# One pool of PSUM banks for matrix products and transposes beside the attention of a two-layer decoder trunk

## The chip, the cores and the metric

The kernel runs on one core of one Trainium2 chip. The metric is the device time of one execution in microseconds (us); three executions of the kernel before took 2252.82, 2257.99 and 2261.49 us, so its median is 2257.99 us.

## What is computed

Two layers (DEPTH 2) work on 1024 tokens of width 1024. Cut to what matters here, a layer is:

```
u   = x * (1 + scale) + shift
A, B, C inputs, gates and merge logits = u W_in
A: GLU -> depthwise conv(31) -> LayerNorm -> swish, times SiLU(A_gate), -> W_a_out = y_a
B: Bg * conv3(Cg * xb), times SiLU(B_gate), -> W_b_out = y_b
C: causal attention of 8 heads on low-rank q and kv, times SiLU(C_gate), -> W_c_out = y_c
m   = sum_i sigmoid(merge_i) * y_i
x   = LayerNorm(alpha * x + gate * (m W_o))
```

The attention of a head is softmax(q k^T * scale) v with a causal mask. All large products are made from a high and a low part of each operand, as three matmuls of 512 columns for each 128 rows of the sum.

## The kernel before, in words

Everything is held transposed (channels on the 128 partitions, tokens along the free axis) and cut into two halves of 512 tokens, h = 0 and h = 1. Each layer has three phases, and `phase` (L1177) closes the PSUM pool and opens it again with another layout at each. Phase 0 makes the large input products and the convolutions. Phase 1 is the attention of the first half of the tokens, beside the output products of the branches B and A of that half. Phase 2 is the attention of the second half; beside it lie the C products of the first half (`merge_jobs`, tile `yps`, L1034), the products with W_o (`wo_jobs`, tile `ops`, L1091), the LayerNorm of the first half (`ln_jobs`, L1094) and the B and A products of the second half. The two phases with attention are the ones that the change touches.

The attention of a head and half (`att_jobs`, L873) has four kinds of jobs. A score job (L904) makes one 128-query block of scores in a bank of tag `st`, takes its maximum on VectorE (L919), the exponential on ScalarE (L921) and divides by the sum (L922, L923), which gives the tile `prob`. A flip job (L928) takes one bank of tag `tp` (tile `tps`), transposes three or four 128x128 blocks of `prob` into it on TensorE (L938), and `split` copies the bank out as a high part on ScalarE (L129) and a low part on VectorE (L130), tile `pt`. A values job (L947) multiplies `pt` with V into the one bank of tag `av` (tile `avps`, L954), which is held for a whole head. A finish job (L958) adds up and gates the head. A head has 3 flips in phase 1 and 7 in phase 2, so the two layers have 2 x 8 x (3 + 7) = 160.

The products beside it take one bank of tag `pj` each (`chunk`, L164): a `yps` product has 12 matmuls and is read by VectorE (L1025 for B, L1028 for A and C), an `ops` product has 24 and is read by VectorE at L1049. The LayerNorm of a half takes a bank of tag `tp` for the mean (tile `meanps`, L757), which eight VectorE instructions read one after the other (L762), then one of tag `tp` for the variance (tile `qv`, L530) and one of tag `av` for the factor that is applied (tile `rstd`, L545). The A products of the second half wait for this LayerNorm: their inputs `y` (loaded at L1003, split at L132 and L133) lie in the buffers c0 to c3, and these are free only when the LayerNorm has been applied (L1103, L1109) and stored.

The order of the jobs is written out by hand: `blend` (L89) mixes attention jobs and product jobs by their estimated costs, `weave` (L66) spreads the LayerNorm jobs over the products (L1248 to L1256). That is the order of the calls. The Tile framework then orders the instructions of each engine ahead of time, by its own estimates, so that TensorE can take a ready product ahead of a transpose that stands earlier in the order of the calls. Within one tag, though, the banks are given out in the order of the calls: in the program before, the tiles on each bank follow one another in that order. A tile that finds no free bank of its tag waits until the last reader of one is done.

The layouts of the phases give each tag its number of banks, eight in all; a score tile of phase 2 takes two banks:

```
layouts = (dict(pj=3, sd=3, tp=1, av=1), dict(pj=3, st=2, tp=2, av=1), dict(pj=2, st=2, tp=1, av=1))
```

Of the kernel before, what the change touches and what calls it, by code (L numbers as in the profile page):

```python
# [1285 lines left out]
def trunk(nc, tc, *args):  # L1286
    from contextlib import ExitStack
    with ExitStack() as es:
        mk = lambda name, **k: es.enter_context(tc.tile_pool(name=name, **k))
        bufs = dict(tab=1, wr=6, ws=6, tt=1, sp=2, ab=2, w=6, x=2, n=5, sm=8, acc=1)  # L1290

        class Pool:
            def __init__(self, p):
                self.p = p

            def tile(self, shape, dt, tag, name):
                return self.p.tile(shape, dt, tag=tag, name=name, bufs=bufs.get(tag, 1))
        class Banks:

            layouts = (dict(pj=3, sd=3, tp=1, av=1), dict(pj=3, st=2, tp=2, av=1), dict(pj=2, st=2, tp=1, av=1))  # L1300
            stack = None

            def lay_out(self, n):
                if self.stack is not None:
                    self.stack.close()
                self.stack = es.enter_context(ExitStack())
                self.bufs = self.layouts[n]
                self.p = self.stack.enter_context(tc.tile_pool(name="ps", bufs=1, space=PSUM))

            def tile(self, shape, dt, tag, name):  # L1310
                return self.p.tile(shape, dt, tag=tag, name=name, bufs=self.bufs[tag])
        big = Pool(mk("a", bufs=1))
        pools = (mk("const", bufs=1), Pool(mk("w", bufs=1)), big, big, Banks(),
                 mk("dram", bufs=1, space=DRAM))
        Trunk(nc, tc, pools, args[:-1], args[-1]).build()
# [74 lines left out]
```

## Time and profile before

| what | value |
|---|---|
| median of three executions | 2257.99 us |
| the profiled execution's own time | 2257.43 us |
| span of its instructions | 2254.8 us |
| mean granted TensorE clock | 0.977 |
| TensorE (PE) busy | 95% |
| VectorE (DVE) busy | 80% |
| ScalarE (ACT) busy | 50% |
| phases 1 and 2 of layer 0 | about 735 to 1062 us, then products alone |
| phases 1 and 2 of layer 1 | about 1850 to 2160 us, then products alone |

PE is matmul work, PEld the loading of weights, which overlaps it. The granted clock is the share of full speed that TensorE was given. A row of the view of waits says which instruction of an engine waited for the end of which other one, for how long in total, how often, and the longest time. A matmul that writes into a bank and waits for the VectorE instruction that reads the bank last is a wait for a bank.

### The profile page before, as it was taken

Reading aid. Unit: us, or ns where it says so; the run is one execution under the profiler, and the core shown is the slowest. Engines: PE = TensorE matmul, PEld = TensorE weight load, DVE = VectorE, ACT = ScalarE, POOL = GpSimd, SP = SyncE. Lnnn points to the kernel's source line nnn. Section 1 sums busy time; section 2 is a strip of 40 time slices with the busy share of each in tenths; the row PEclk is TensorE's granted clock in tenths of the full one; section 3 lists DMA queues with packets and bytes.
Section 4 is the critical chain, followed back from the end, with each engine's and each line's share of the span. In section 5 each row is a group of like instructions: output and inputs, shape, how many; then the busy total and the mean of one; then the engine's idle time right before and its main releaser. Section 6 shows DMA issues by size and latency. Waiting matters only on the chain.

```text
span 2254.8 us, 29755 instructions
## 1 busy us (share of the span) xinstructions
PE 2139.8 (95%) x10097; PEld 1723.9 (76%) x10097; DVE 1810.3 (80%) x2910; ACT 1138.4 (50%) x2072; POOL 235.6 (10%) x483
## 2 busy tenths in 40 slices
PE   8889999999999989988997999999999999999896
PEld 7668788888778778866775787888887778887686
DVE  4786889899997788787868769899898868867786
ACT  2764443343443756655448544443434447666743
POOL 4010100000001321101001101000000023211000
PEclk9999999999999999997998999999999999999998
DMA  7575642223224986665535757332222269745442
GB/s 265 180 203 189 186 167 100 97 99 103 79 72 125 238 228 187 175 193 173 178 108 189 201 163 207 119 107 89 94 69 67 68 197 221 190 129 141 159 156 64
DMA packets 185191, 336.68 MB, mean 149 GB/s; under 512 B 22608, under 2 KB 47440, under 8 KB 185040
## 3 DMA queue, kind: packets, MB, share of 16 engines
q1 hardware_dynamic: 124560, 218.50, 31.2%
q0 software_dynamic: 46656, 91.12, 15.4%
q10 hardware_dynamic: 13824, 25.17, 3.0%
q8 instruction: 79, 1.29, 0.2%
q14 instruction: 72, 0.59, 0.1%
HBM read 254.16 MB, written 80.54 MB: 148 GB/s over the span
## 4 chain that ended last, share of the span: by engine, by line
PE 75%; issue 11%; DMA 5%; DVE 4%; ACT 3%; POOL 1%; SPq 0%; POOLq 0%; DVEq 0%; ACTq 0%
PE lgps L295 19%; PE bgps L295 7%; PE xgps L295 7%; PE aps L295 7%; PE cgps L295 3%; PE agps L295 3%; PE yps L186 3%; PE yps L187 3%; PE yps L188 3%; PE avps L954 3%; PE tps L938 3%; PE ops L186 2%; PE score L914 2%; PE ops L187 2%; PE ops L188 2%
## 5 line engine op out<-in xcount | busy, mean ns | idle before, releaser
L295 PE MATMUL lgps<-u,wsplit 128*128 128x512 f32 x2016 | 483.9, 397 | 13.7 <-ACT lgps L260 12.0
L295 PEld LDWEIGHTS lgps<-u,wsplit 128*128 128x128 f32 x2016 | 379.8, 189 | 108.3 <-ACT lgps L260 13.8
L129 ACT CAST wsplit<-wraw 128x512 fp32r<-128x512 f32 (+1 forms) x524 | 318.3, 615 | 270.7 <-DVE wraw L220 54.8
L130 DVE TENSOR_TENSOR wsplit<-wraw,wsplit 128x512 fp32r<-128x512 f32 (+1 forms) x524 | 353.5, 679 | 71.2 <-ACT wsplit L129 67.8
L736 DVE SCALAR_TENSOR_TENSOR cacc<-abuf,vec,cacc 128x1024 f32<-128x1024 f32 x240 | 306.9, 1279 | 0.6
L295 PE MATMUL xgps<-u,wsplit 128*128 128x512 f32 x672 | 160.4, 397 | 0.0
L295 PE MATMUL bgps<-u,wsplit 128*128 128x512 f32 x672 | 160.0, 397 | 0.0
L295 PE MATMUL aps<-u,wsplit 128*128 128x512 f32 x672 | 158.1, 395 | 0.0
L295 PEld LDWEIGHTS xgps<-u,wsplit 128*128 128x128 f32 x672 | 126.0, 188 | 31.6 <-issue 1.4
L295 PEld LDWEIGHTS bgps<-u,wsplit 128*128 128x128 f32 x672 | 126.0, 188 | 31.5 <-issue 1.4
L295 PEld LDWEIGHTS aps<-u,wsplit 128*128 128x128 f32 x672 | 126.2, 188 | 30.6
L130 DVE TENSOR_TENSOR pt<-tps,pt 128x512 fp32r<-128x512 f32 (+1 forms) x160 | 100.9, 634 | 36.9 <-ACT pt L129 35.8
L129 ACT CAST pt<-tps 128x512 fp32r<-128x512 f32 (+1 forms) x160 | 85.7, 540 | 77.2 <-PE tps L938 74.8
L954 PE MATMUL avps<-pt,Vh 128*128 128x256 f32 x640 | 120.5, 303 | 1.7 <-ACT pt L129 1.2
L919 DVE TENSOR_REDUCE nm<-score 128x1 f32<-128x384 f32 (+7 forms) x128 | 95.8, 751 | 30.8 <-PE score L917 30.2
L186 PE MATMUL yps<-y,wsplit 128*128 128x512 f32 x256 | 107.4, 422 | 12.4 <-ACT y L132 6.2
L921 ACT ACTIVATE prob<-score,nm 128x384 f32<-128x384 f32 (+7 forms) x128 | 94.3, 740 | 46.0 <-PE tps L938 25.0
L186 PE MATMUL ops<-m,wsplit 128*128 128x512 f32 (+1 forms) x320 | 114.8, 359 | 0.0
L188 PE MATMUL ops<-m,wsplit 128*128 128x512 f32 (+1 forms) x320 | 112.8, 353 | 0.0
L187 PE MATMUL ops<-m,wsplit 128*128 128x512 f32 (+1 forms) x320 | 112.6, 352 | 0.0
L938 PE MATMUL tps<-cs,prob 128*128 128x128 f32 x576 | 93.1, 279 | 18.0 <-DVE pt L130 17.5
L954 PEld LDWEIGHTS avps<-pt,Vh 128*128 128x128 f32 x640 | 95.6, 195 | 14.2 <-ACT pt L129 7.4
(322 smaller groups left out, 4253.9 us busy)
## 6 DMA issues: line engine op xcount, KB each, us to landing
wraw<-in_win SPq DMA_DIRECT2D x264, 256.0 KB, 2.7
wraw<-in_wout SPq DMA_DIRECT2D x96, 256.0 KB, 3.0
mt<-tD SPq DMA_DIRECT2D x96, 256.0 KB, 4.4
adaraw<-in_wada SPq DMA_DIRECT2D x64, 256.0 KB, 3.3
wraw<-in_wo SPq DMA_DIRECT2D x64, 256.0 KB, 3.0
tD<-mt ACTq DMA_DIRECT2D x48, 256.0 KB, 2.0
Kh<-knD POOLq DMA_DIRECT2D x48, 256.0 KB, 5.1
Vh<-vD POOLq DMA_DIRECT2D x48, 256.0 KB, 5.7
```

The costliest lines, as they stand in the source:

```text
L129: nc.scalar.copy(dst[:, 0], src)
L130: nc.vector.tensor_tensor(dst[:, 1], src, dst[:, 0].bitcast(F32), op=ALU.subtract)
L186: mm(ps, w[:, 0, c], x[k][:, 0, cols], start=k == 0, stop=False)
L187: mm(ps, w[:, 0, c], x[k][:, 1, cols], start=False, stop=False)
L188: mm(ps, w[:, 1, c], x[k][:, 0, cols], start=False, stop=k == n - 1)
L295: mm(ps, w[:, a, c], x[:, e], start=n < 2 and k == 0 and i == 0, stop=k == 3 and i == 2, skip_group_check=True)
L736: nc.vector.scalar_tensor_tensor(acc, a[:, k:k + S], w, acc, op0=ALU.mult, op1=ALU.add)
L914: mm(o, q[0:96, 0, qc], k[0:96, 0, :w], start=True, stop=False)
L919: nc.vector.tensor_reduce(nm[:, 0:1], sp[:, :nk], axis=AX.X, op=ALU.max, negate=True)
L921: nc.scalar.activation(p[:, :nk], sp[:, :nk], AF.Exp, bias=nm[:, 0:1], accum_out=nm[:, 1:2])
L938: nc.tensor.transpose(tp[:, c:c + P], st["p", hd, 2 * half + b][:, (2 * kp + k) * P:(2 * kp + k + 1) * P], self.ident)
L954: mm(av[:, half * 256:(half + 1) * 256], v[:, 2 * kp + k], pt[:, w, (1 - k) * 256:(2 - k) * 256], start=kp == 0 and k == 0 and w == 0, sto ...
```

## The change

In the two layouts with attention the tags `pj` and `tp` become one tag of as many banks as the two had together: 3 + 2 = 5 in phase 1, 2 + 1 = 3 in phase 2. A request for a tag that the layout does not have (`tp`) is served from `pj`. Phase 0 keeps its layout. No instruction is added or removed.

```diff
-            layouts = (dict(pj=3, sd=3, tp=1, av=1), dict(pj=3, st=2, tp=2, av=1), dict(pj=2, st=2, tp=1, av=1))
+            layouts = (dict(pj=3, sd=3, tp=1, av=1), dict(pj=5, st=2, av=1), dict(pj=3, st=2, av=1))
             stack = None
@@
             def tile(self, shape, dt, tag, name):
+
+                tag = tag if tag in self.bufs else "pj"
                 return self.p.tile(shape, dt, tag=tag, name=name, bufs=self.bufs[tag])
```

## Rows read from the trace of the kernel before

**Rows 1.** Stretches: length, busy PE, PEld, DVE, ACT, POOL (instructions), granted clock, DMA share, GB/s.
```profile
735.00:845.00 110.00, 100.22 (x553) 82.24 (x554) 82.67 (x172) 71.57 (x170) 34.16 (x75) 0.95 0.90 234
845.00:945.00 100.00, 99.00 (x557) 82.16 (x557) 81.19 (x139) 63.74 (x112) 15.94 (x34) 1.00 0.70 186
945.00:985.00 40.00, 32.39 (x173) 26.27 (x172) 29.40 (x49) 20.35 (x36) 4.58 (x10) 0.97 0.66 174
985.00:1010.00 25.00, 22.15 (x117) 17.00 (x116) 20.77 (x41) 14.05 (x25) 1.41 (x3) 0.91 0.59 189
1010.00:1060.00 50.00, 40.33 (x185) 32.93 (x185) 36.93 (x68) 31.54 (x50) 6.35 (x13) 0.76 0.51 163
...
1850.00:1938.00 88.00, 86.81 (x489) 71.53 (x490) 69.45 (x149) 63.71 (x156) 29.48 (x65) 0.96 0.94 229
1938.00:2060.00 122.00, 120.10 (x664) 99.33 (x665) 86.01 (x143) 78.48 (x137) 19.58 (x41) 1.00 0.57 152
2060.00:2110.00 50.00, 47.65 (x252) 36.61 (x251) 40.79 (x70) 32.17 (x56) 4.89 (x11) 1.00 0.49 140
2110.00:2135.00 25.00, 18.02 (x84) 13.84 (x83) 18.99 (x32) 18.73 (x32) 1.38 (x3) 0.80 0.49 158
```

**Rows 2.** Waits of PE, 725 to 1110 us (layer 0): total, times, longest.
```profile
PE tps L938 <- DVE pt L130: 10.0, 7, 3.3
PE yps L186 <- DVE mt L1028: 6.1, 1, 6.1
PE yps L186 <- DVE mf L1025: 5.4, 1, 5.4
PE score L914 <- ACT prob L921: 5.3, 5, 2.4
...
PE score L914 <- DVE gt L795: 1.4, 1, 1.4
```

**Rows 3.** Waits of PE, 1845 to 2255 us (layer 1).
```profile
PE tps L938 <- DVE pt L130: 7.5, 7, 3.3
...
PE yps L186 <- DVE mt L1028: 2.4, 2, 1.4
...
PE avps L954 <- ACT pt L129: 1.2, 2, 0.9
```

**Rows 4.** Busy time by stretch of the transposes' instructions (tile tps) alone, without POOL.
```profile
971.00:989.00 18.00, 0.00 (x0) 0.22 (x1) 0.00 (x0) 0.00 (x0) 0.82 0.45 113
...
2071.00:2082.00 11.00, 0.00 (x0) 0.00 (x0) 0.00 (x0) 0.00 (x0) 1.00 0.19 39
```

**Rows 5.** Timeline, 1026 to 1036 us: consecutive transposes and their copies (start, us).
```profile
1027.74 0.59 ACT L129 CAST pt<-tps 128x512 fp32r<-128x512 f32 x1 [3.94 <-PE tps L938]
1028.36 0.69 DVE L130 TENSOR_TENSOR pt<-tps,pt 128x512 fp32r<-128x512 f32 x1 [1.89 <-ACT pt L129]
...
1029.10 1.12 PE L938 MATMUL tps<-cs,prob 128*128 128x128 f32 x4 [0.76 <-DVE pt L130]
...
1033.91 0.87 PE L938 MATMUL tps<-cs,prob 128*128 128x128 f32 x3 [3.27 <-DVE pt L130]
```

**Rows 6.** Groups of instructions, 735 to 1062 us: busy, mean ns, idle before.
```profile
L923 ACT ACTIVATE prob<-prob,nm 128x128 f32<-128x128 f32 (+3 forms) x64 | 48.0, 774 | 5.4 <-DVE nm L922 5.4
L919 DVE TENSOR_REDUCE nm<-score 128x1 f32<-128x128 f32 (+3 forms) x64 | 47.8, 750 | 14.3 <-PE score L917 14.0
...
L921 ACT ACTIVATE prob<-score,nm 128x128 f32<-128x128 f32 (+3 forms) x64 | 47.2, 740 | 27.5 <-PE tps L938 13.6 <-DVE nm L919 13.6
L130 DVE TENSOR_TENSOR pt<-tps,pt 128x512 fp32r<-128x512 f32 (+1 forms) x74 | 46.5, 632 | 13.0 <-ACT pt L129 12.6
L938 PE MATMUL tps<-cs,prob 128*128 128x128 f32 x268 | 44.1, 283 | 10.0 <-DVE pt L130 10.0
L129 ACT CAST pt<-tps 128x512 fp32r<-128x512 f32 (+1 forms) x74 | 39.6, 540 | 35.9 <-PE tps L938 35.5
...
L1028 DVE SCALAR_TENSOR_TENSOR mt<-mt,yps 128x512 f32<-128x512 f32 x19 | 13.0, 684 | 3.5 <-PE yps L188 2.7 <-DMA mt<-tD 0.8
```

## The prediction

> **What bounds the kernel now.** I read the busy time by stretch first [rows 1]. TensorE is the engine to save: in the stretches up to 945 us in layer 0 and up to 2060 us in layer 1 it is busy for 91 to 99% of the time. It falls off later in phase 2: 32.4 of 40 us, 22.2 of 25, 40.3 of 50 in layer 0, and 47.7 of 50 and 18.0 of 25 in layer 1. Over these five stretches 7.6 + 2.8 + 9.7 + 2.3 + 7.0 = 29.4 us are idle, and in three of them the granted clock is 0.91, 0.76 and 0.80, so that part of the work ran at 1.2 instead of 2.4 GHz right after such idle time.
>
> The view of waits then says what TensorE waited for. The first row of either layer is the same: a transpose waits until VectorE has read the bank of the transposes before, 10.0 us in 7 waits and 7.5 us in 7 [rows 2, 3]. That is a wait for a bank, since `pt` itself lies in four other buffers. The timeline shows one turn of the single `tp` bank of phase 2: four transposes, the ScalarE copy (0.59 us), the VectorE copy (0.69), and the next transposes only after that [rows 5]. From one ScalarE copy to the transposes that follow it are 1.36 us; with the transposes ahead of it (0.87 to 1.12 us here) the bank turns in some 2.4 us when nothing is late. A head has 7 flips in phase 2, so 17 us of the 27 us that a head has (217 us from 845 to 1062, by 8) go through this one bank at the least.
>
> Something is late, though. The mean of the LayerNorm takes the same bank, and in 18 us of layer 0 and 11 us of layer 1 not one transpose runs [rows 4]. TensorE passes that time with products of branch B, which stand later in the order of the calls. Then these run out, as the A products wait for the LayerNorm, whose `qv` stands in the queue for the same bank behind the transposes held up, and whose `rstd` waits for the `avps` bank of a head that is late for the same reason. The stretches after it, 1010 to 1060 and 2110 to 2135 us, are the worst of all.
>
> **The change, part by part.** It adds and removes no instruction and no DMA, so the sum is about waits alone.
>
> *Phase 1* goes from 3 + 2 banks to 5. The transposes hardly lacked a bank there: in 1850 to 1938 us TensorE is busy for 86.8 of 88 us [rows 1]. One wait of a product for its bank, 6.1 us at the end of phase 1 in layer 0 [rows 2], could profit from banks that no flip needs any more. I take it with the product waits below.
>
> *Phase 2, transposes.* With three banks the turn of one bank no longer sets the pace of the flips; the next thing late is a copy, at 0.54 us on ScalarE and 0.63 on VectorE per flip [rows 6], or the softmax. The bank waits of 17.5 us bound the gain from above. From below I bound it at nothing, as each could become a wait for the copy (like the 1.2 us of the values in layer 1 [rows 3]) or for the softmax (5.3 us in layer 0 [rows 2]). I take 60%, -10.5 us: nearer to the upper end, because the waits for this bank are nearly three times the others.
>
> *Phase 2, products.* They waited 6.1 + 5.4 + 2.4 = 13.9 us for a bank [rows 2, 3]. A third bank lets one more product start, but while the mean holds one bank of the three, two are left, as before, and the flips now want them too. Bounds: 0 and -13.9; I take -3, near the lower end, for VectorE is what is late behind the 5.4 us.
>
> *The clock.* The time lost to the lower level is at most the idle share of the clock times the busy time: 0.24 x 40.3 + 0.09 x 22.2 + 0.20 x 18.0 = 15.3 us [rows 1]. If about half of the idle time goes, I expect half of this back: -7.5 (bounds 0 and -15.3).
>
> *What the shared tag costs.* Within a tag the banks are given out in the order of the calls. So a product can no longer start ahead of a transpose that stands before it; it waits until that transpose has its `prob`. The trace before has no such wait. The nearest rows are the two stretches without a transpose: products and other work kept TensorE busy in the 18 us less the 5.4 us of the wait inside, and in the 11 us [rows 2, 4], 23.6 us together. If all of that stood still the cost would be +23.6; if the flips are ready when their turn comes it is nothing. In the stretch after the mean, though, the transposes start 0.05 us after the copy that frees the bank (28.36 + 0.69 against 29.10 [rows 5]), so their `prob` lay ready. I take +4. The queues behind: VectorE and ScalarE are in order, and copies of flips now come in groups of up to three, which is in the 60% above.
>
> *The borders of the phases.* Banks lie elsewhere after the change, so the first scores wait for another tile of phase 0; the one such wait is 1.4 us [rows 2]. I take 0, between -1.4 and +1.4, as phase 0's last gates cover it.
>
> Sum: -10.5 - 3 - 7.5 + 4 + 0 = -17.0 us. The profiled execution took 2257.4 us, which is 0.6 below the median of the three, so 2240.4 and, on the median, **2241 us**.
>
> **The rivals.** *No change, 27%: the banks were not it.* Each bank wait becomes a wait for the copy or the softmax, and VectorE, busy for 37 of the 50 us from 1010 [rows 1], is what is late. Then a fifth of the transposes' waits goes (-3.5) and the clock stays: 2254 us. For it: the 5.4 us of a product are VectorE's lateness. Against it: the flips lined up behind one bank, and ScalarE waited 35.5 us for transposes before its copies [rows 6]. A measured case of the Trainium skill speaks for this rival ("TensorE: Matmul & The Clock Gate", section "HAM oscillation — how this bites in real kernels"): double-buffering PSUM gave a kernel with long sums no further gain (125.5 against 126.6 us). By that rule the time here would stay at 2258. It fits the products, whose 12 or 24 matmuls outlast the 0.68 us of their read [rows 6], not the flips, whose three or four transposes at 0.28 us are over before the two copies of 0.54 and 0.63 are.
>
> *Slower, 15%: products queue behind transposes that are not ready.* Place: the start of each head, in both phases with attention. The softmax of a block after its scores takes 0.75 + 0.74 + 0.77 us for maximum, exponential and division [rows 6], 2.26 us; today TensorE fills that with a product. There are 2 x 2 x 8 = 32 heads, 72 us if nothing fills it. Scores and values still fill most. It decides from 17 / 32 = 0.53 us of unfilled time per head; at 1 us per head it is +32 - 17: 2273 us. Against it: phase 1 with its two banks for flips had the same softmax to wait for, and TensorE was at 99% there in layer 1 [rows 1].
>
> *Much faster, 8%.* All waits for banks go, the LayerNorm comes early enough for the A products, and the clock holds: -17.5 - 6 - 15 = 2219 us.
>
> *The change does not do what it says:* two of the three banks always hold products and one is left for flips, which is the layout before. It gives 2258 and lies in the 27%.
>
> **How the numbers follow.** The forecast of a gain through the free bank has 50%, with a range of its own of 2228 to 2250 us. The range that is to hold 8 in 10 leaves out the upper half of the slower case and the lower part of the much faster one: 2218 to 2266. A measurement of this kernel can tell 0.5%, 11.3 us, from no change: faster is below 2246.7, slower above 2269.3. Faster: most of the 50%, the 8% and a little of the 27%, 0.57. Slower: the 15% and a tail of the order in which the framework lays the instructions anew, which I can't work out, 0.17. Same: 0.26.
>
> **What would show it.** Right: the waits of `tps` for `pt` are down by more than half in both layers; transposes run while the mean is read; the span from the mean to the factor of the LayerNorm is shorter; the clock after 1010 us is above 0.9. The 60% is wrong if waits of the values for `pt` or of scores for `prob` take the place of the bank waits. The +4 is wrong if TensorE shows waits ahead of products for `prob`, or idles at the start of each head. The forecast as a whole is wrong if phase 2 is no shorter though the bank waits have gone, or if phase 1, which has nothing to gain, grows.

## The result, and the profile after

The changed kernel takes 2232.03 us (median of four executions, 2226.85 to 2233.02) against 2255.89 us for the kernel before in the same sessions (2252.82 to 2261.49): a ratio of 0.9897 with a 95% interval of 0.9879 to 0.9916, or 23.9 us less. The profiled executions have spans of 2230.0 and 2254.8 us, 24.8 us apart. That is faster by more than 0.5%, inside the range, and inside the forecast's own range of 2228 to 2250 us; the gain was forecast at 17 us.

Where it came from is read from the busy time by stretch, cut at the same events in both runs: the first score of a layer, the end of the last head of phase 1, the first read of the LayerNorm's mean, the end of the last head of phase 2, the last read of a product (each taken from the first and last instructions of the tiles `score`, `avps`, `meanps` and `yps`). Columns as in [rows 1]. The kernel before, nine stretches from the first score of layer 0 on:

```profile
735.90:821.60 85.70, 82.91 (x481) 68.66 (x482) 66.68 (x146) 62.22 (x153) 30.96 (x68) 0.98 0.92 233
821.60:971.80 150.20, 140.89 (x768) 115.91 (x767) 116.53 (x197) 87.79 (x152) 22.52 (x48) 0.98 0.73 197
971.80:1078.60 106.80, 88.83 (x433) 70.04 (x431) 80.52 (x143) 58.00 (x96) 8.39 (x18) 0.86 0.55 170
1078.60:1104.10 25.50, 25.50 (x114) 20.59 (x114) 23.11 (x41) 10.67 (x18) 0.00 (x0) 1.00 0.61 196
1104.10:1845.60 741.50, 719.82 (x3090) 571.93 (x3088) 617.55 (x902) 343.59 (x598) 47.30 (x89) 0.99 0.40 127
1845.60:1933.10 87.50, 84.09 (x481) 69.63 (x482) 67.12 (x147) 62.44 (x153) 31.10 (x69) 0.96 0.93 229
1933.10:2071.50 138.40, 135.49 (x740) 111.16 (x739) 100.16 (x163) 86.76 (x152) 22.43 (x47) 1.00 0.60 159
2071.50:2160.80 89.30, 79.88 (x416) 61.93 (x416) 67.61 (x116) 58.13 (x97) 4.05 (x10) 0.94 0.44 140
2160.80:2188.90 28.10, 26.71 (x123) 21.56 (x122) 25.49 (x43) 15.06 (x26) 0.00 (x0) 1.00 0.58 194
```

The changed kernel, the same stretches:

```profile
740.40:825.90 85.50, 83.70 (x481) 69.31 (x482) 67.03 (x146) 62.39 (x153) 30.80 (x68) 0.96 0.93 233
825.90:971.50 145.60, 139.30 (x763) 116.02 (x762) 116.63 (x197) 86.76 (x152) 22.77 (x49) 0.98 0.75 201
971.50:1064.90 93.40, 82.29 (x414) 66.86 (x413) 77.67 (x140) 56.33 (x94) 8.12 (x17) 0.89 0.59 187
1064.90:1095.90 31.00, 31.00 (x138) 25.15 (x138) 26.39 (x46) 11.80 (x20) 0.00 (x0) 1.00 0.63 201
1095.90:1836.10 740.20, 720.03 (x3090) 572.52 (x3088) 616.99 (x901) 343.78 (x598) 47.23 (x89) 0.99 0.41 127
1836.10:1921.90 85.80, 83.73 (x481) 69.42 (x482) 66.72 (x147) 62.30 (x153) 30.95 (x69) 0.96 0.91 233
1921.90:2057.30 135.40, 133.93 (x739) 111.44 (x738) 99.69 (x163) 86.38 (x152) 22.65 (x48) 1.00 0.60 163
2057.30:2132.00 74.70, 70.96 (x400) 58.41 (x399) 64.13 (x112) 55.25 (x94) 3.72 (x9) 1.00 0.50 157
2132.00:2163.70 31.70, 31.19 (x143) 25.37 (x141) 28.27 (x48) 16.69 (x28) 0.00 (x0) 1.00 0.63 197
```

Phase 1 is the same within 2 us (85.7 and 85.5, 87.5 and 85.8). Phase 2 up to the mean gains 4.6 and 3.0 us. The stretch from the mean to the last head gains 13.4 and 14.6 us, and the products left over after it, 114 matmuls before and 138 now in layer 0, take 5.5 and 3.6 us of that back. The rest of a layer (741.5 and 740.2) does not move.

In sum the two phases of both layers take 711.5 us before and 683.1 after, 28.4 us less. That is more than the 24.8 us of the spans, because the profiled execution of the changed kernel comes to its first score 4.5 us later (740.4 against 735.9 us), in work that the change does not touch. Over the thirteen profiled executions of this study the first score lies between 735.3 and 740.4 us; in the changed kernel run again it lies at 736.6 us.

The waits of TensorE in layer 0, 725 to 1110 us, after (total, times, longest):

```profile
PE score L914 <- ACT prob L921: 6.2, 2, 4.2
PE yps L186 <- DVE mt L1028: 5.9, 1, 5.9
PE tps L938 <- DVE pt L130: 2.3, 1, 2.3
```

and in layer 1, 1820 to 2230 us:

```profile
PE avps L954 <- ACT pt L129: 1.9, 3, 0.8
...
PE score L914 <- ACT prob L921: 1.4, 1, 1.4
PE yps L186 <- DVE mt L1028: 1.0, 1, 1.0
```

The waits of transposes for their bank were the first row in both layers, 10.0 and 7.5 us [rows 2, 3]; now 2.3 us are left in layer 0 and no such row in layer 1. The waits of products for `mf` (5.4 us) are gone too, those for `mt` are not. In the stretches in which the mean is read, where no transpose ran [rows 4], the tile `tps` alone now shows:

```profile
971.50:996.60 25.10, 3.23 (x18) 2.53 (x18) 2.46 (x4) 2.68 (x5) 0.86 0.53 148
2057.30:2072.80 15.50, 2.18 (x14) 1.77 (x14) 1.93 (x3) 1.62 (x3) 1.00 0.45 130
```

18 and 14 transposes run beside the mean. The mean itself is held longer than before, since its eight reads on VectorE now stand between the copies of flips. The reads of layer 0 and of layer 1 before, then after (the last two numbers ahead of the shapes are the starts of the first and of the last read):

```profile
L762 DVE SCALAR_TENSOR_TENSOR r<-meanps,r x8: 681/684/694, 971.8 to 987.4; 128x512 f32<-128x512 f32 x8
L762 DVE SCALAR_TENSOR_TENSOR r<-meanps,r x8: 681/684/692, 2071.5 to 2081.3; 128x512 f32<-128x512 f32 x8
...
L762 DVE SCALAR_TENSOR_TENSOR r<-meanps,r x8: 670/681/691, 971.5 to 996.0; 128x512 f32<-128x512 f32 x8
L762 DVE SCALAR_TENSOR_TENSOR r<-meanps,r x8: 664/680/690, 2057.3 to 2072.1; 128x512 f32<-128x512 f32 x8
```

From the first start to the last end these are 16.3 and 10.5 us before, 25.1 and 15.5 after.

### The profile page after: what moved, and what is told of

Read it like the earlier page. It is cut to its first block, busy times and chain, and to the rows that moved or that the text cites. A ratio compares the mean times of both kernels' runs of the same rounds, so it can differ in the third digit from the quotient of the medians.

```text
span 2230.0 us, 29769 instructions
## 1 busy us (share of the span) xinstructions
PE 2136.2 (96%) x10097; PEld 1730.9 (78%) x10097; DVE 1809.0 (81%) x2910; ACT 1135.0 (51%) x2072; POOL 235.0 (11%) x483
## 4 chain that ended last, share of the span: by engine, by line
PE 76%; issue 14%; DMA 4%; DVE 3%; ACT 2%; POOL 1%; SPq 0%; POOLq 0%; DVEq 0%; ACTq 0%
PE lgps L295 18%; PE bgps L295 7%; PE xgps L295 7%; PE aps L295 7%; PE cgps L295 4%; PE agps L295 3%; PE yps L186 3%; PE avps L954 3%; PE yps L187 3%; PE yps L188 3%; PE tps L938 3%; PE ops L186 2%; PE ops L187 2%; PE ops L188 2%; PE score L914 2%
## 5 line engine op out<-in xcount | busy, mean ns | idle before, releaser
L295 PEld LDWEIGHTS lgps<-u,wsplit 128*128 128x128 f32 x2016 | 381.0, 189 | 109.9 <-ACT lgps L260 13.9
L186 PE MATMUL yps<-y,wsplit 128*128 128x512 f32 x256 | 111.6, 436 | 4.8 <-ACT y L132 4.2
L954 PE MATMUL avps<-pt,Vh 128*128 128x256 f32 x640 | 110.9, 297 | 3.2 <-ACT pt L129 2.1
L187 PE MATMUL yps<-y,wsplit 128*128 128x512 f32 x256 | 104.0, 406 | 0.2 <-DVE y L133 0.2
L129 ACT CAST wsplit<-wt 128x512 fp32r<-128x512 f32 x112 | 69.5, 620 | 68.0 <-DVE wt L220 47.8
```

The lines of the kernel that those rows point to most:

```text
L129: nc.scalar.copy(dst[:, 0], src)
L186: mm(ps, w[:, 0, c], x[k][:, 0, cols], start=k == 0, stop=False)
L187: mm(ps, w[:, 0, c], x[k][:, 1, cols], start=False, stop=False)
L295: mm(ps, w[:, a, c], x[:, e], start=n < 2 and k == 0 and i == 0, stop=k == 3 and i == 2, skip_group_check=True)
L954: mm(av[:, half * 256:(half + 1) * 256], v[:, 2 * kp + k], pt[:, w, (1 - k) * 256:(2 - k) * 256], start=kp == 0 and k == 0 and w == 0, sto ...
```

## The experiments

My theory: the gain is in phase 2, and it is the one bank of the flips, which is free more often when three are shared; both the turn of this bank (some 2.4 us a flip) and the mean that holds it count. The rivals: the products gain by more banks (in phase 1 or 2); the order alone does it, since products can no longer run ahead; or the mean's hold is all of it.

**One phase at a time.** Only the layout of one phase is changed; the other stays as before.

```diff
-dict(pj=5, st=2, av=1), dict(pj=3, st=2, av=1))
+dict(pj=3, st=2, tp=2, av=1), dict(pj=3, st=2, av=1))    # phase 2 only
+dict(pj=5, st=2, av=1), dict(pj=2, st=2, tp=1, av=1))    # phase 1 only
```

> Phase 1 keeps 3 + 2 separate banks, phase 2 has the shared three. Theory (the gain is the one bank of the flips in phase 2): 2232 us, between 2226 and 2238, a ratio of 0.987 to 0.992 to the kernel before. Rival (the five shared banks of phase 1 give a good part, since the products after the attention get them): half of the gain is gone, some 2244 us.

> Only phase 1 shares its banks, phase 2 keeps 2 + 1. Theory: nothing to gain and little to lose, 2256 us within 5. Rival (phase 1 gives part of the gain): some 2244 us. The two runs with one phase each should add up to the whole change, -24 us.

Phase 2 alone: 2231.78 us against 2255.26, a ratio of 0.9885 (0.9862 to 0.9908). Phase 1 alone: 2254.59 us, 1.0003 (0.9989 to 1.0018). The two add up to the whole change; phase 1 gives nothing and costs nothing.

**Two shared banks.** Phase 2 has one bank less than before, and the shared tag.

```diff
-dict(pj=3, st=2, av=1))
+dict(pj=2, st=2, av=1))
```

> Like the changed kernel, but phase 2 has two shared banks and one bank stays unused. Theory (banks): the flips and products held some 0.8 and 1.1 banks on average in phase 2 of the kernel before, so two banks are full and this is slower than the kernel before, 2280 us or more. Rival (order: the shared tag stops products from running ahead and keeps them for the end of the attention, and that is the gain): still faster than before, 2245 us or less.

2263.25 us, 1.0032 (1.0021 to 1.0043). Neither: with one bank less the shared order gives no gain (what it is worth with three banks this run cannot tell; the next one bears on it), but I had put the price of the bank much too high. Two shared banks are only 8 us worse than three separate ones. The waits of TensorE from 725 us on, both layers:

```profile
PE avps L954 <- ACT pt L129: 10.3, 7, 3.6
...
PE yps L186 <- DVE mt L1028: 7.1, 3, 5.8
...
PE yps L186 <- DVE pt L130: 3.7, 5, 1.3
PE tps L938 <- DVE pt L130: 3.5, 6, 1.5
...
PE tps L938 <- DVE mf L1025: 2.3, 3, 1.1
```

The values now wait 10.3 us for copies (1.2 before), and the four waits for banks shown are 16.6 us together, where those for `pt`, `mt` and `mf` were 17.5 + 8.5 + 6.1 us before. Two new rows cross over: products wait for the copies of flips, and flips for the reads of products.

**Two banks for flips, one for products.** Still separate, as before.

```diff
-dict(pj=2, st=2, tp=1, av=1))
+dict(pj=1, st=2, tp=2, av=1))
```

> The layout before, but phase 2 has two banks for flips and LayerNorm and one for products, all separate. Theory (the gain is banks for the flips, and sharing is what makes them free for it): the waits of transposes go, products wait for their single bank instead, about 2262 us. Rival (a second product bank is worth little, because attention work lies between the products): 2240 us or less, and sharing is not needed.

2269.99 us, 1.0073 (1.0051 to 1.0095). The waits of TensorE, both layers:

```profile
PE yps L186 <- DVE mt L1028: 24.7, 21, 5.8
PE ops L186 <- DVE r L1049: 16.5, 23, 1.1
...
PE tps L938 <- DVE pt L130: 3.0, 4, 1.1
```

The transposes' waits go from 17.5 to 3.0 us, and the products wait 24.7 + 16.5 us for their one bank. When they wait decides what this means. From the first score to the end of the last head, layers 0 and 1:

```profile
739.70:1057.90 318.20, 299.86 (x1655) 246.66 (x1655) 260.82 (x483) 205.38 (x399) 61.87 (x134) 0.97 0.76 210
1850.40:2149.80 299.40, 289.86 (x1615) 239.81 (x1616) 230.73 (x421) 204.01 (x399) 57.52 (x126) 0.98 0.69 179
```

That is 617.6 us, against 657.9 in the kernel before and 620.4 in the changed kernel, which by then has done the same matmuls (1655 and 1616 in its rows). While there are flips, two banks for them and one for the products are as good as the pool. The loss comes after the last head, as the layout of phase 2 stays in force until the next phase: the products left over take 41.7 and 43.6 us instead of 25.5 and 28.1, and what follows them up to the next layer or the end 829.2 us instead of 807.4. Of the 41.2 us of waits 34.5 lie there; from 2150 us on, in layer 1:

```profile
PE ops L186 <- DVE r L1049: 10.0, 15, 1.1
PE yps L186 <- DVE mt L1028: 9.7, 9, 1.6
```

So two rivals fall for the time of the attention: the products need no third bank there, not even a second one, and no shared order is needed for the gain, since the tags are separate here. What the pool adds is that its banks pass to the products when the flips are over. A layout with separate tags that changes after the last head was not run.

**The mean in a product bank.** The layout before; in phase 2 the tiles `meanps` and `qv` come from `pj`, so that `tp` serves flips alone.

```diff
+                if self.bufs is self.layouts[2] and name in ("meanps", "qv"):
+                    tag = "pj"
```

> The layout before, but in phase 2 the mean and the variance of the LayerNorm take a product bank, so the one bank of the flips serves flips alone. Theory (the bank's turn of 2.4 us paces the flips everywhere): about a third of the gain, 2248 us, with waits of transposes for pt of 8 us or more still there. Rival (the LayerNorm blocking the flips is all of it): 2235 us or less, and the waits of transposes nearly gone.

2242.45 us, 0.9940 (0.9919 to 0.9962): about half of the gain, more than I had expected, less than the rival. 18 transposes run beside the mean in layer 0, and the waits of transposes fall to 6.6 us over both layers. The products have one bank for that time; whether this or the turn of the flips' bank keeps the other half is not separated.

**The mean copied out of its bank.** The layout before, one more ScalarE copy in phase 2, and the eight reads go to the copy.

```diff
             nc.tensor.matmul(st["ps"], self.ones, st["tot"], start=True, stop=True)
+            if self.ps.bufs is self.ps.layouts[2]:
+                mean = self.t2("w", "meansb", c)
+                nc.scalar.copy(mean, st["ps"])
+                st["ps"] = mean
```

> The layout before with its one separate bank for the flips, and in phase 2 the mean of the LayerNorm copied out of that bank by one more ScalarE instruction. Theory (what stopped the flips for 18 and 11 us was the hold of the mean, about half of the gain): 2243 us, like the run with the mean in a product bank (2242.5). Rival (that run gained by the other order of its products, not by the hold): 2250 us or more.

2236.29 us, 0.9906 (0.9886 to 0.9927), 20.3 us less than the 2256.58 beside it: more than expected. The instructions of the tile `meansb` in this run (its line numbers from L757 on are four higher):

```profile
L760 ACT COPY meansb<-meanps x3: 372/567/567, 975.2 to 2198.5; 128x512 f32<-128x512 f32 x2, 128x256 f32<-128x256 f32 x1
```

The third of them belongs to the last LayerNorm, after the attention.

The transposes alone in the same run, in the stretches in which the mean had stopped them, by busy time:

```profile
971.80:989.00 17.20, 2.29 (x14) 1.62 (x14) 2.54 (x4) 2.02 (x4) 1.00 0.68 208
2061.80:2073.00 11.20, 1.65 (x11) 1.30 (x11) 1.23 (x2) 1.05 (x2) 1.00 0.48 154
```

And its waits of TensorE for transposes' and products' banks, both layers:

```profile
PE tps L942 <- DVE pt L130: 10.6, 7, 3.3
...
PE yps L186 <- DVE mt L1032: 7.1, 2, 6.2
...
PE yps L186 <- DVE mf L1029: 2.1, 2, 1.8
```

A copy of 0.57 us frees the bank, and with 10.6 of the 17.5 us of waits for the bank's turn still there, most of the gain is made. The eight reads of the copy take as long as those of the bank did (median 682 and 684 ns in layer 0), so it is not that they are faster. So the hold of the mean was the larger part, and the turn of the bank the smaller.

**The mean copied out of a shared bank.** The same edit on the changed kernel.

> The changed kernel, and in phase 2 the mean of the LayerNorm is copied out of its bank by one more ScalarE instruction, so that the bank is held for some 2 us instead of 25 and 15. Theory (while the mean holds a bank two are left, and the run with two shared banks shows what a bank is worth: 31 us over two phases 2 of some 215 us each): 40 us of holding give 3 us back, 2229 us. Rival (in those 40 us VectorE and ScalarE are late, not the banks): 2232 or slower by the copies.

> The changed kernel again, beside the next one: 2232 us, a ratio of 0.988 to 0.991.

> The changed kernel with the mean copied out, again, beside the changed kernel on the same chip. Theory (a shared bank held for 40 us by a mean is worth some microseconds): 3 to 7 us faster than the run beside it. Rival (the 7 us of the first run lay in the spread of the runs): within 2 us of it.

First run: 2224.59 us, 0.9869 (0.9846 to 0.9892). Again, on one chip: the changed kernel 2229.02 us, 0.9875 (0.9856 to 0.9895); with the copy 2224.35 us, 0.9854 (0.9838 to 0.9870). The two intervals overlap, but all eight executions with the copy (2222.22 to 2225.75) lie below all eight without (2226.85 to 2233.02). It is the fastest version of the study, some 5 us ahead of the changed kernel.

That the hold of a shared bank is the reason is not shown. In layer 0 ScalarE waits for the load of the tile `xr` (L1043) just while the mean is held, and does the exponentials of earlier scores only after that; the next scores of TensorE wait for these. The changed kernel, then the second run with the copy:

```profile
976.64 0.63 ACT L1043 ACTIVATE xr<-xr 128x512 f32<-128x512 f32 x1 [7.20 <-DMA xr<-in_xT]
978.83 0.80 PE L914 MATMUL score<-Kh,Qh 96*128 96x512 f32 x1 [4.21 <-ACT prob L921]
...
971.65 0.63 ACT L1047 ACTIVATE xr<-xr 128x512 f32<-128x512 f32 x1 [1.09 <-DMA xr<-in_xT]
973.84 0.50 PE L918 MATMUL score<-Kh,Qh 96*128 96x512 f32 x1 [0.33 <-ACT prob L925]
```

With the copy the wait of TensorE shrinks from 4.2 to 0.3 us, which is most of the 5 us, and no run separates it from the bank. The same wait for `xr` stands in the kernel before:

```profile
976.05 0.63 ACT L1043 ACTIVATE xr<-xr 128x512 f32<-128x512 f32 x1 [6.44 <-DMA xr<-in_xT]
```

There it lengthens the hold itself: VectorE waits 3.9 us of the 16.3 for the squares that stand behind it on ScalarE.

In that series the four kernels make a table (medians, us; the executions of one kernel spread over 2 to 8 us):

| | mean held in its bank | mean copied out |
|---|---|---|
| banks separate (2 + 1) | 2256.6 | 2236.3 |
| three shared banks | 2229.0 | 2224.4 |

The pool is worth 27.6 us while the mean holds a bank, and 11.9 us when it does not. So some 16 of its 27.6 us go with the hold; by the spread of the executions I estimate this to be good to about 4 us, and part of it can be the wait for `xr`, which is shorter with the copy in both rows (in layer 0 3.0 us instead of 6.4, 1.1 instead of 7.2). Between the two runs with the copy the transposes' waits fall from 10.6 us to

```profile
PE tps L942 <- DVE pt L130: 2.3, 1, 2.3
```

That is 8.3 us beside the 11.9: the turn of the one bank.

**The LayerNorm's factor from the pool.** On the changed kernel, alone and with the mean copied out.

```diff
+                if self.bufs is self.layouts[2] and name == "rstd":
+                    tag = "pj"
```

> The changed kernel, and in phase 2 the factor of the LayerNorm (rstd) also comes from the shared banks instead of the bank of the attention's values, for which it waits in both layers until a head ends (23.4 and 15.2 us lie between qv and rstd). Theory (after the change the LayerNorm still ends late, and the A products and their idle time with it): rstd some 10 us earlier, 3 to 6 us gained, about 2228 us. Rival (the products of branch B now last until the LayerNorm is done anyway): no change, 2232, or a little slower, since rstd holds a shared bank for 6 us.

> The changed kernel with both edits: rstd from the shared banks and the mean copied out. Theory: the gains add up, about 2225 us. Rival: 2232 us or the better of the two alone.

Alone 2229.23 us, 0.9894 (0.9871 to 0.9917); both 2228.76 us, 0.9889 (0.9869 to 0.9909). The rival holds: no change from the changed kernel in the first. The second is even 4.2 us slower than the copy alone, and its four executions (2227.33 to 2230.11) lie above the four of that run (2223.40 to 2225.75). The factor and its use by VectorE in layer 0, with the factor from the pool, by tile:

```profile
L545 PE MATMUL rstd<-rsrow,onesr x1: 628/628/628, 1009.5 to 1009.5; 128*128 128x512 f32 x1
...
L1103 DVE TENSOR_TENSOR r<-r,rstd x8: 676/677/689, 1010.1 to 1028.2; 128x512 f32<-128x512 f32 x8
```

The use in the changed kernel:

```profile
L1103 DVE TENSOR_TENSOR r<-r,rstd x8: 676/677/687, 1023.9 to 1028.7; 128x512 f32<-128x512 f32 x8
```

The factor starts at 1009.5 us instead of 1023.4, and the first use follows, but the last of the eight starts at 1028.2 against 1028.7: VectorE reaches them among its other work at the same time. In layer 1 the last use does start earlier, at 2093.7 instead of 2100.0 us. Over the two phases of both layers nothing comes of it, 682.8 us against 683.1, and with the mean copied out 677.8 against 678.7. The wait that I took away was covered.

The loss lies after the last product of layer 1, where the last LayerNorm uses the same layout: that end takes 70.1 and 70.2 us with the factor from the pool, 66.3 and 66.2 without, and TensorE waits 3.4 us there before the matmul that makes the factor, a wait that is not in the other two. My rival had the price in the wrong place: the factor holds a shared bank for 19 us in layer 0, not 6, as its eight uses too stand among other work, and this cost nothing that can be seen.

## Why the prediction was right, point by point

*Phase 2, transposes (-10.5).* The waits went from 17.5 to 2.3 us, -15.2; they did not turn into waits for the copies (2.9 us of the values over both layers, 1.2 before) or for the softmax (7.6 us, 6.5 before). The step's size, 60%, was too careful. Its account of them was off in weight: I put the turn of the bank first, but by the table some 16 of 27.6 us go with the mean's hold, and taking the hold away alone gives 20.3 us. The hold was in the reading of [rows 4], and had no term of its own. One reading was wrong without touching the sum: the heads of phase 2 in layer 0 run from 834.3 us (the first score) to 1078.6, not from 845 to 1062, so a head has about 31 us and not 27.

*Phase 2, products (-3).* 5.4 + 0.6 us for `mf` and 1.6 of the 8.5 us for `mt` went, -7.6 on the 14.5 us of both layers, against -3 on 13.9. The wait of 6.1 us at the end of phase 1, which I counted as a possible gain of phase 1, is still 5.9 us. My reason for the low end was right, the low end was not: VectorE was late behind the 5.4 us, and this wait went with the mean's hold rather than by a third bank for products. With the mean copied out and still two banks for products, the same rows are 7.1 + 2.1 us, 5.3 less.

*The clock (-7.5).* By the same recipe the loss to the lower level is now: 945 to 985 us 0.09 x 35.4, 985 to 1010 us 0.03 x 22.7, 1010 to 1060 us 0.12 x 45.4, and none in layer 1, where the granted clock is 1.00 from the mean on:

```profile
945.00:985.00 40.00, 35.38 (x186) 28.95 (x185) 29.49 (x53) 25.89 (x46) 4.57 (x10) 0.91 0.71 183
985.00:1010.00 25.00, 22.70 (x128) 18.31 (x127) 23.82 (x46) 16.81 (x28) 1.41 (x3) 0.97 0.54 166
1010.00:1060.00 50.00, 45.39 (x226) 37.09 (x226) 41.75 (x72) 29.66 (x50) 6.71 (x14) 0.88 0.64 215
```

3.2 + 0.7 + 5.4 = 9.3 us, against 15.3 and 1.0 for the stretch from 945 us that I had left out. TensorE's busy time in the two phases of both layers, for the same work, fell from 664.3 to 656.1 us, by 8.2. So the term was about right, and so is the recipe, within about 2 us. Over the whole program the busy time fell by 3.6 us only (2139.8 to 2136.2), because 4.8 us more lie ahead of the first score in that execution. Of the signs that I had named, the clock after 1010 us above 0.9 is the one that missed: it is 0.88 in layer 0.

*The shared tag (+4).* The waits of scores for `prob` grew by 1.1 us, and the longest is 4.2 us in layer 0, beside the mean; that one follows ScalarE's wait for `xr` and is no price of the shared tag. I take the 24 matmuls more after the last head of layer 0 to be products that TensorE no longer runs ahead. They cost nothing there, as TensorE is busy for 31.0 of 31.0 us.

*The sum.* The waits named here make -15.2 - 7.6 + 1.1 = -21.7 us; TensorE's whole idle time in the two phases fell by 20.2 us (47.2 to 27.0), its busy time by 8.2, and that is the 28.4 us. The 3.6 us lost outside the phases in the profiled pair are in no term. The steps were the right ones, and three were mis-sized: the two bank terms by 9.3 us together too small, as the hold was not priced, and the shared tag by 2.9 too dear. All these errors go the same way, so none of them hid another.

*The rivals.* Slower by products behind unready transposes: phase 1, where it would have shown first, is unchanged. No change, because waits move to the copies: they did not, with three banks; with two, they do (10.3 us). The measured case of the Trainium skill that spoke for this rival ("TensorE: Matmul & The Clock Gate", section "HAM oscillation — how this bites in real kernels": double-buffering PSUM gave no further gain there) does not carry over, and not even to the products, for which I had let it stand: with one bank instead of two they wait 41.2 us, most of it when no flip lies between them.

## What to carry to other kernels

Ask of a bank not only how long its users fill it, but how long its last reader keeps it: a tile that eight instructions read in turn stopped every flip behind it for 18 us, and one copy of 0.57 us out of its bank gave 20.3 us where the pool gave 27.6. A pool with one tag lets a bank go to whoever needs it next, at the price that tiles start in the order of the calls. With the mean left in its bank three shared banks took 2232 us and the better split into separate ones 2256; two shared banks were nearly worth three separate ones. Judge a split by stages: the one with a single bank for products was as fast as the pool up to the last head, and lost more than that gain after it. Before a late step is moved, look whether the engine that uses it would take it up any sooner.

## What was not expected

Two shared banks cost only 8 us against three separate ones, where I had expected 25 or more. In the changed kernel the mean keeps its bank for longer, 25.1 and 15.5 us against 16.3 and 10.5, and the stretch is faster all the same. While the attention lasts, one bank is enough for the products; they need more of them when nothing else is left to run. And a load that ScalarE waits for, 6 to 7 us in layer 0, stands behind a wait of TensorE of 5.4 us before and of 4.2 us after the change, though TensorE itself waits for no DMA there.
